# Second layer's experts: the body behind a turn's first branch takes the output products' PSUM banks (sc) instead of the gather's (ob) and the places' (md)

## The chip, the core and the metric

The kernel runs on one core of a Trainium2 chip. Its time is the device time of one execution in microseconds (us). TensorE (PE in the rows) multiplies and transposes into PSUM, eight banks of 128 partitions by 512 fp32 values; VectorE (DVE) and ScalarE (ACT) read the banks; GpSimd (POOL) takes no part in the stretch spoken of here; SyncE (SP) issues the weight loads.

## The reference

Two layers of a hybrid block over 256 latent tokens and 256 context tokens of width 1024. In each layer a mixer of four head groups is followed by a mixture of 16 experts, of which a router gives each token two. The part that matters:

```
for e in range(N_EXPERTS):                       # 16
    a = jax.nn.silu(h @ w_gate[e]) * (h @ w_up[e])
    y = y + gates[..., e:e + 1] * (a @ w_down[e])   # gates are 0 for all but 2 experts of a token
```

`w_gate` and `w_up` are 1024 x 512, `w_down` 512 x 1024, all fp32: 6 MB an expert. In the second layer only the 256 latent tokens go through the experts.

## The kernel before, in words

An expert's tokens are counted on the chip and put into blocks of 64 slots (`BLK`). The second layer (`turns()` within `moe`, lines 1864 to 1933) runs sixteen turns, one expert each, in an order written out by hand on all engines. Every engine reads the expert's count into a register (`cv`). A turn does, in this order on TensorE:

1. the input product of the first block (`mm_in`, L1544, into a bank of tag pj), with the additions of the turn before last (`add`, L1597, tag ob, read by VectorE at L1606) between its parts; ScalarE makes the SiLU of it (`act`, L1550) and VectorE multiplies by the gate (L1551);
2. the first branch, L1882: if the expert has more than 64 tokens, its body gathers a second block (`fetch`, L1515) and makes the input product and the activation of it;
3. in the first twelve turns a quarter of the gather of four experts' first blocks that come later (`four_fetch`, L1100, tag ob), copied out by ScalarE or VectorE;
4. a matmul that finds the places of the block's tokens (`where`, L1575, tag md), compared on VectorE (L1576);
5. four transposes of the activated block (`spin`, L1557, tag tp), copied by ScalarE (L1558);
6. the output product of the turn before (`mm_out`, L1568, tag sc), scaled on VectorE and split on ScalarE and VectorE (`parts`, L1582 to L1587);
7. the second branch, L1920, whose body finishes a second block.

The banks are taken from a pool by tag, in rotation within a tag: `BANKS = {"tp": 1, "md": 1, "pj": 2, "sc": 2, "ob": 2}`, all eight. Semaphores are laid by the framework from what the program's text uses, body or not: who takes a bank after the branch waits for the last reader in the body. Where the body is skipped, each engine, as it comes past the branch, raises its semaphore by what the body would have raised, and does so in its own order, behind the work that it had before the branch.

The weights come in six loads of 1 MB a turn (L183), issued by SyncE as soon as their buffer is free, turns ahead.

Of the kernel before, what the change touches and what calls it, by code (L numbers as in the profile page):

```python
# [123 lines left out]
def hybrid_block_kernel(ctx: ExitStack, tc: tile.TileContext, xin, const, fconst, par, fpar, misc, fng,  # L124
# [12 lines left out]
    def bank(tag="tp"):  # L137
        return psp.tile([P, 512], F32, name="b_" + tag, tag=tag, bufs=BANKS[tag])
# [120 lines left out]
    def C(name, a=0, b=None):  # L259
        at, n = CONST[name]  # L260
        return cst[:, at + a:at + (n if b is None else b)]
# [21 lines left out]
    def copy(dst, src):  # L283
        rr["n"] += 1
        if rr["n"] % 2:
            nc.scalar.activation(dst, src, AF.Copy)
        else:
            nc.vector.tensor_copy(dst, src)
# [796 lines left out]
    def four_onehots(dst, pd, g):  # L1085

        for t in range(dst.shape[1]):
            nc.vector.tensor_tensor(dst[:, t], C("iota")[:, None, :BLK].to_broadcast([P, 4, BLK]),
                                    pd[:, t].rearrange("p (i r) -> p i r", r=4)[:, :, 3 - g:4 - g].to_broadcast([P, 4, BLK]),
                                    op=OP.is_equal)  # L1090
# [305 lines left out]
    def moe(l, cnt, idx, gc, pd, pk, rk, hx, h0, hp):  # L1396
# [5 lines left out]
        with ExitStack() as mctx:  # L1402
# [27 lines left out]
            b = bank()  # L1430
# [61 lines left out]
            def onehot(e, cols, off=None, name=None, into=None):  # L1492

                qs = []
                for t in range(T):
                    q = into[t] if into else ew.tile([P, cols.shape[1]], F32R, name=f"{name}{t}", bufs=1)
                    if off is None:
                        V.tensor_scalar(q, cols, pd[:, t, e:e + 1], None, op0=OP.is_equal)
                    else:
                        V.tensor_scalar(q, cols, off, pd[:, t, e:e + 1], op0=OP.add, op1=OP.is_equal)  # L1500
                    qs.append(q)
                return qs
# [1 line left out]
            def to_slots(h, b):  # L1504
                copy(h.rearrange("p k s -> p (k s)"), b)

            def fetch(oh):

                h = rp.tile([P, 8, BLK], F32, name="hO", tag="h0")
                for j in range(4):  # L1510
                    b = bank("ob")
                    for k in range(2):
                        at = (2 * j + k) * P
                        for i in range(2 * T):
                            nc.tensor.matmul(b[:, k * 256:(k + 1) * 256], lhsT=hx[i % 2][:, i // 2, at:at + P],  # L1515
                                             rhs=oh[i // 2], start=(i == 0), stop=(i == 2 * T - 1))
                    copy(h[:, 2 * j:2 * j + 2], b.rearrange("p (k s) -> p k s", s=256)[:, :, :BLK])
                return h
# [17 lines left out]
            def mm_in(w, h, s0=0, tag="pj", between=None, b=None, ks=range(8)):  # L1536
                b = bank(tag) if b is None else b
                for k in ks:
                    if between:
                        between(k)  # L1540
                    for j in range(2):
                        at = (k % 2) * D + j * 512
                        x = h[k // 4][:, k % 4] if isinstance(h, list) else h[:, k, s0:s0 + BLK]
                        nc.tensor.matmul(b[64 * j:64 * j + 64], lhsT=x,  # L1544
                                         rhs=w[k // 2][:, at:at + 512],
                                         start=(k == 0), stop=(k == 7), tile_position=(0, 64 * j))
                return b

            def act(b, gate, a):
                nc.scalar.activation(a[64:], b[:64], AF.Silu)  # L1550
                V.scalar_tensor_tensor(a[64:], a[64:], gate[64:], b[64:], op0=OP.mult, op1=OP.mult)  # L1551
                return a
# [37 lines left out]
            def add(*blocks, only=None, last=False, banks=None):  # L1590

                for t in range(T) if only is None else only:
                    for h in range(2):
                        cs = slice(h * 512, (h + 1) * 512)
                        b = banks[h] if banks else bank("ob")
                        for i, (st, ohT) in enumerate(blocks):
                            nc.tensor.matmul(b, lhsT=ohT[:, t * P:(t + 1) * P], rhs=st[h],  # L1597
                                             start=(i == 0), stop=(i == len(blocks) - 1))
                        if last:
                            pool = h and t < T - 1  # L1600
                            y = AM[2] if pool and t % 2 == 0 else HE[1].rearrange("p k s -> p (k s)")[:, cs]
                            V.tensor_mul(y, b, g2[t // 2][:, cs])
                            (nc.gpsimd if pool else V).tensor_tensor(xres[t][:, cs], xres[t][:, cs], y, op=OP.add)
                        else:
                            y = xres[t] if l else ACC[t]
                            V.tensor_tensor(y[:, cs], b, y[:, cs], op=OP.add)  # L1606
# [68 lines left out]
            w = aT = owed = None  # L1675
# [184 lines left out]
            def next_count(p):  # L1860

                return nc.values_load(cnt[0:1, TURNS[p]:TURNS[p] + 1], engines=engs, min_val=0, max_val=N)

            def turns():

                w = aT = owed = before = None
                oh1 = onehot(TURNS[0], C("iota2"), off1, name="on")
                cv = next_count(0)  # L1870
                for p, e in enumerate(TURNS):
                    last = p == NE - 1
                    now, nxt = four[p // 4 % 2], four[(p // 4 + 1) % 2]
                    pw, pT, w = w, aT, [main.take("exp", l, 6 * e + q) for q in range(6)]
                    x = [q[:, :, p % 4] for q in now[0]]

                    a1, t1, st1, o1 = AM[(p + 1) % 2], AT[(p + 1) % 2], ST[(p + 1) % 2], OT[(p + 1) % 3]
                    if p % 4 == 0 and p < NE - 4:
                        four_onehots(nxt[1], pd, p // 4 + 1)
                    b0 = mm_in(w, x, between=lambda k: owed and k in (4, 6) and add(owed, only=[k // 2 - 2]))  # L1880
                    a0 = act(b0, gc[:, 0, e:e + 1], AM[p % 2])
                    with tc.If(cv > BLK):  # L1882
                        act(mm_in(w, fetch(oh1), tag="md"), gc[:, 1, e:e + 1], a1)
                    if last:
                        any_ = nc.values_load(cnt[0:1, 16:17], engines=engs, min_val=0, max_val=N)
                    else:
                        main.done(4, 2 if p else 0)
                        onehot(TURNS[p + 1], C("iota2"), off1, into=oh1)
                        if p < NE - 4:
                            four_fetch(nxt[0], hx, nxt[1], [p % 4])  # L1890
                        ncv = next_count(p + 1)
                    o = where(e, OT[p % 3], C("slot", 0, 1), "md")
                    aT = spin(a0, AT[p % 2])
                    if p:
                        b = mm_out(pw, pT, bank("sc"))
                        main.done(2)
                        owed = parts(b, ST[p % 2]), before

                    def second():
                        where(e, o1, C("slot", 1, 2), "md")  # L1900
                        add((parts(mm_out(w, spin(a1, t1)), st1), o1))

                    if last:
                        b = mm_out(w, aT, bank("sc"), lambda f: f > 1 and add(owed, only=[f - 2]))

                        owed = parts(b, st1), o
                        st1 = ST[p % 2]
                        with tc.If(any_ > BLK):
                            with tc.If(cv > BLK):
                                second()  # L1910
                            for q in range(NE):
                                ce = nc.values_load(cnt[0:1, q:q + 1], engines=engs, min_val=0, max_val=N)
                                with tc.If(ce > P):
                                    for i in range(6):
                                        nc.sync.dma_start(w[i], source("exp", l, 6 * q + i))
                                    overflow(q, w, ce, P, a1, t1, st1, o1, into=oh1)
                        add(owed)
                        main.done(6)
                        break
                    with tc.If(cv > BLK):  # L1920
                        second()
                    cv, before = ncv, o
# [215 lines left out]
```

## Time and profile before

| | |
|---|---|
| runs shown | 1346.06, 1339.88, 1345.20 us; median 1345.2 |
| profiled execution | 1349.27 us, of which the span from the first to the last instruction is 1347.1 |
| TensorE busy in the span | 1151.7 us (85%) |
| second layer's experts | from 1060.9 us, the first input product, to about 1338 |
| mean granted TensorE clock | 0.916 |

The time of the profiled execution is 4.1 us over the median of the three runs. Times in rows are us from the start of the span. A line number is that of the kernel's file; most operations of a turn are recorded at the line of a helper. [...] A window's row gives its stretch and length, then busy us and the count of instructions of TensorE, its weight loads, VectorE, ScalarE and GpSimd, and behind them the granted clock, the mean busy share of the 16 DMA engines and GB/s. In a row, `[0.73 <-ACTq L1882]` says that the engine stood idle for 0.73 us before it, and what ended that: here ScalarE's sequencer at the branch.

### The profile page before, as it was taken

The numbers are of one execution on the slowest core, as the hardware profiler recorded it, in microseconds if no ns is written. First come the engines' busy times: TensorE is split into PE (matmuls) and PEld (weight loads), VectorE is DVE, ScalarE is ACT, GpSimd is POOL, SyncE is SP. The second block draws the span as 40 slices with busy tenths as digits, with TensorE's granted clock in tenths as the row PEclk, the third lists the DMA queues.
The fourth block names the chain that finished last, engine by engine and source line by source line (L and its number), as shares of the span: only waits on it lengthen the run. The fifth ranks groups of instructions, "written<-read, shape, count | busy, mean of one in ns | idle before, by whom it ended". The sixth has DMA issues, their size and how long they took to land. (4 is left out here: it accounts for less than half of the span.)

```text
span 1347.1 us, 16575 instructions
## 1 busy us (share of the span) xinstructions
PE 1151.7 (85%) x6205; PEld 644.7 (48%) x6205; DVE 538.8 (40%) x1070; ACT 314.9 (23%) x569; POOL 294.1 (22%) x238
## 2 busy tenths in 40 slices
PE   6799998887899879978898995788878899989984
PEld 2456565556688433323233333667667533333321
DVE  4431967335423530110010038486535444433444
ACT  2422233222222121011111115314424111111111
POOL 4332232222024111111111045534315000000000
PEclk9999998888799788989999996989869899999997
DMA  9485442412571787499999836121136399976951
GB/s 363 181 321 189 157 179 97 146 63 95 217 267 67 287 351 245 128 387 391 384 394 392 327 111 225 63 94 48 63 156 258 123 402 420 418 287 256 420 200 49
DMA packets 48559, 310.61 MB, mean 231 GB/s; under 512 B 6017, under 2 KB 6209, under 8 KB 14096
## 3 DMA queue, kind: packets, MB, share of 16 engines
q1 hardware_dynamic: 41936, 292.77, 55.9%
q0 software_dynamic: 6320, 15.27, 4.4%
q8 instruction: 91, 1.49, 0.4%
q10 hardware_dynamic: 144, 0.52, 0.1%
q14 instruction: 68, 0.56, 0.1%
HBM read 297.99 MB, written 12.32 MB: 230 GB/s over the span
## 5 line engine op out<-in xcount | busy, mean ns | idle before, releaser
L603 POOL TENSOR_TENSOR ws<-w,ws 128x1024 fp32r<-128x1024 f32 x50 | 121.1, 2436 | 218.2 <-ACT ws L602 200.6
L1544 PE MATMUL b_pj<-w,HE 128*64 128x512 f32 x416 | 109.7, 664 | 23.8 <-issue 19.3
L234 PE MATMUL b_pj<-hh,ws 128*128 128x512 f32 (+1 forms) x448 | 122.2, 362 | 1.4 <-POOL ws L603 1.4
L1568 PE MATMUL b_sc<-w,rows 128*64 128x512 f32 x448 | 109.7, 634 | 0.6 <-ACT rows L1558 0.6
L693 DVE SCALAR_TENSOR_TENSOR cacc<-gl,pr,cacc 128x512 f32<-128x512 f32 (+1 forms) x120 | 91.8, 765 | 2.6
L234 PEld LDWEIGHTS b_pj<-hh,ws 128*128 128x128 f32 x448 | 79.5, 198 | 21.1 <-issue 9.7
L234 PE MATMUL b_pj<-hl,ws 128*128 128x512 f32 (+1 forms) x224 | 78.3, 350 | 0.0
L1544 PEld LDWEIGHTS b_pj<-w,HE 128*64 128x64 f32 x416 | 34.6, 150 | 85.7 <-issue 82.5
L602 ACT ACTIVATE ws<-w 128x1024 fp32r<-128x1024 f32 x50 | 52.5, 1052 | 70.2 <-PE b_pj L234 44.6
L277 POOL TENSOR_TENSOR rf<-rf,half 128x1 f32<-128x1 f32 x2 | 1.1, 553 | 300.3 <-DVE rf L276 300.3
L1568 PEld LDWEIGHTS b_sc<-w,rows 128*64 128x64 f32 x448 | 32.7, 145 | 63.5 <-issue 60.7
L1606 DVE TENSOR_TENSOR x<-b_ob,x 128x512 f32<-128x512 f32 x68 | 44.0, 687 | 43.7 <-PE b_ob L1597 43.6
L1451 POOL DMA_INDIRECT sums<-y,rws x19 | 29.8, 1567 | 137.4 <-DVE y L1450 122.3
L1551 DVE SCALAR_TENSOR_TENSOR X<-X,gc,b_pj 64x512 f32<-64x512 f32 x16 | 12.1, 754 | 109.2 <-ACT X L1550 109.2
L1544 PE MATMUL b_pj<-w,hf 128*64 128x512 f32 x224 | 54.0, 619 | 0.9 <-PEq L1920 0.5
L234 PE MATMUL b_md<-w,sT 128*32 128x256 f32 x704 | 53.8, 430 | 1.3 <-DVE mT L313 1.3
L1544 PE MATMUL b_pj<-w,x 128*64 128x512 f32 x224 | 52.9, 601 | 1.0 <-PEq L1920 0.6
L1450 DVE COPY y<-b_sc 128x512 f32<-128x512 f32 x15 | 10.4, 692 | 102.1 <-PE b_sc L1568 61.9
L1597 PE MATMUL b_ob<-st,ohT 128*128 128x512 f32 x76 | 33.1, 504 | 18.9 <-DVE st L1587 11.9
L234 PEld LDWEIGHTS b_pj<-hl,ws 128*128 128x128 f32 x224 | 44.5, 199 | 5.2
L1550 ACT ACTIVATE X<-b_pj 64x512 f32<-64x512 f32 x16 | 9.4, 589 | 158.8 <-PE b_pj L1544 151.2
L1456 POOL DMA_INDIRECT G<-hbuf,idx x15 | 15.2, 1016 | 110.8 <-PE b_ob L1528 61.7
(475 smaller groups left out, 2062.4 us busy)
## 6 DMA issues: line engine op xcount, KB each, us to landing
w<-in_exps_dram SPq DMA_DIRECT2D x168, 1024.0 KB, 12.1
w<-in_ada_dram SPq DMA_DIRECT2D x48, 1024.0 KB, 4.9
w<-in_win_dram SPq DMA_DIRECT2D x16, 1024.0 KB, 6.0
hold<-in_exps_dram SPq DMA_DIRECT2D x12, 1024.0 KB, 18.5
w<-in_wout_dram SPq DMA_DIRECT2D x8, 1024.0 KB, 4.8
hf<-in_exps_dram SPq DMA_DIRECT2D x6, 1024.0 KB, 4.7
cst<-in_exps_dram SPq DMA_DIRECT2D x6, 1024.0 KB, 9.2
pr<-in_par_dram SPq DMA_DIRECT2D x2, 1461.5 KB, 6.2
```

What stands on the lines that cost most here:

```text
L234: nc.tensor.matmul(out_, lhsT=lhsT, rhs=rhs, **kw)
L602: nc.scalar.activation(wh[:, :n], src, AF.Copy)
L603: nc.gpsimd.tensor_tensor(wl[:, :n], src, wh[:, :n].bitcast(F32), op=OP.subtract)
L693: nc.vector.scalar_tensor_tensor(ac, gl[:, :, j:j + L], R("cvw", i * 31 + j, i * 31 + j + 1), ac, op0=OP.mult, op1=OP.add)
L1450: V.tensor_copy(y, b)
L1451: nc.gpsimd.indirect_dma_start(out=sums[:, :], out_offset=bass.IndirectOffsetOnAxis(ap=row, axis=0), in_=y, in_offset=None, bounds_check=1 ...
L1456: nc.gpsimd.indirect_dma_start(out=g, out_offset=None, in_=hbuf[:, :], in_offset=bass.IndirectOffsetOnAxis(ap=ix, axis=0), bounds_check=N ...
L1544: nc.tensor.matmul(b[64 * j:64 * j + 64], lhsT=x, rhs=w[k // 2][:, at:at + 512], start=(k == 0), stop=(k == 7), tile_position=(0, 64 * j))
L1551: V.scalar_tensor_tensor(a[64:], a[64:], gate[64:], b[64:], op0=OP.mult, op1=OP.mult)
L1568: nc.tensor.matmul(b[64 * j:64 * j + 64], lhsT=aT[:, f, :], rhs=w[4 + f // 2][:, at:at + 512], start=(f == 0), stop=(f == 3), tile_positio ...
L1597: nc.tensor.matmul(b, lhsT=ohT[:, t * P:(t + 1) * P], rhs=st[h], start=(i == 0), stop=(i == len(blocks) - 1))
L1606: V.tensor_tensor(y[:, cs], b, y[:, cs], op=OP.add)
```

## The change

`fetch` gets a tag for its banks, and the body of the first branch in `turns()` gives it sc, for the gather and for the input product behind it. The other caller of `fetch`, for a third block of an expert, keeps ob.

```
-            def fetch(oh):
+            def fetch(oh, tag="ob"):

                 h = rp.tile([P, 8, BLK], F32, name="hO", tag="h0")
                 for j in range(4):
-                    b = bank("ob")
+                    b = bank(tag)
...
                     with tc.If(cv > BLK):
-                        act(mm_in(w, fetch(oh1), tag="md"), gc[:, 1, e:e + 1], a1)
+                        act(mm_in(w, fetch(oh1, "sc"), tag="sc"), gc[:, 1, e:e + 1], a1)
```

The order of instructions stays the same on every engine; what each waits for does not. On TensorE, in turn 3, right behind the first branch (a row is a line, an operation, output and inputs, the output's size; `hxh` and `hxl` are the two halves of the tokens, `ohs` the one-hot choice, `pick` and `pdT` the places' inputs; the names in brackets are the semaphores waited for, DVE, PE, Activation and the load queues):

```order
 L1882 UNCONDITIONAL_BRANCH [waits PE_49]
-L1100 MATMUL b_ob<-ohs,hxh 128x256 [waits DVE_49,PE_49,Activation_49]
+L1100 MATMUL b_ob<-ohs,hxh 128x256 [waits DVE_49]
...
 L1862 TENSOR_LOAD cnt
-L1575 MATMUL b_md<-pdT,pick 128x256 [waits DVE_49,Activation_49]
-L1557 MATMUL b_tp<-cst 128x64 x4
-L1568 MATMUL b_sc<-w,rows 64x512 [waits DMAHW5_49]
+L1575 MATMUL b_md<-pdT,pick 128x256
+L1557 MATMUL b_tp<-cst 128x64 [waits DVE_49]
+L1557 MATMUL b_tp<-cst 128x64 x3
+L1568 MATMUL b_sc<-w,rows 64x512 [waits DMAHW5_49,DVE_49,PE_49]
```

The gather keeps one wait, for an addition of VectorE ahead of the branch; the places' matmul has none left; the transposes now carry the wait for the activation, and the output product takes on the wait for the branch. Turns 13 to 16 read the same, without the gather.

On VectorE, at the same branch in turn 1, the body's own operations (`hO` is the gathered block, `cst` the activated one, `gc` the gates):

```order
 L1882 COMPARE_AND_BRANCH
-L288 COPY hO<-b_ob 128x128 x2
-L1551 SCALAR_TENSOR_TENSOR cst<-cst,gc,b_md 64x512
+L288 COPY hO<-b_sc 128x128 x2
+L1551 SCALAR_TENSOR_TENSOR cst<-cst,gc,b_sc 64x512
 L1882 UNCONDITIONAL_BRANCH x2
 L1500 TENSOR_SCALAR on_11681<-cst,off_11667,pd 128x256
```

Nothing but the banks that they read has moved there; on ScalarE it is the same, and GpSimd and SyncE have no difference.

## Rows read from the trace of the kernel before

**Rows 1.** Windows: us, busy and count per engine, clock, DMA share, GB/s.

```profile
1093.05:1108.16 15.11, 14.22 (x65) 5.41 (x65) 6.61 (x11) 2.83 (x5) 0.00 (x0) 1.00 0.98 392
...
1194.60:1222.84 28.24, 23.29 (x92) 8.26 (x90) 11.90 (x19) 4.47 (x8) 0.00 (x0) 0.88 0.43 173
...
1253.07:1268.18 15.11, 14.22 (x65) 5.41 (x65) 7.22 (x12) 2.23 (x4) 0.00 (x0) 1.00 1.01 420
1268.18:1284.71 16.53, 14.74 (x57) 4.79 (x57) 6.62 (x11) 2.23 (x5) 0.00 (x0) 0.90 1.01 418
1284.71:1301.23 16.52, 14.74 (x57) 4.79 (x57) 6.62 (x11) 2.23 (x4) 0.00 (x0) 0.90 0.72 282
1301.23:1316.06 14.83, 13.04 (x57) 4.39 (x57) 6.62 (x11) 2.24 (x5) 0.00 (x0) 1.00 0.01 2
1316.06:1338.18 22.12, 13.94 (x45) 4.69 (x45) 9.78 (x15) 4.30 (x7) 0.00 (x0) 0.79 0.08 25
```

**Rows 2.** List of waits from 1055 us: total us, times, longest us.

```profile
PE b_ob L1100 <- ACTq L1882: 8.1, 11, 0.8
...
PE b_md L1575 <- DVEq L1882: 6.5, 4, 1.6
...
PE b_pj L1544 <- PEq L1920: 1.3, 8, 0.2
...
PE b_pj L1544 <- DMA w<-in_exps_dram: 0.6, 4, 0.2
```

**Rows 3.** Timeline of turn 3: start us, us, engine, line, operation, count, idle before.

```profile
1091.07 1.94 PE L1544 MATMUL b_pj<-w,hf 128*64 128x512 f32 x8
1093.05 0.59 ACT L1550 ACTIVATE cst<-b_pj 64x512 f32<-64x512 f32 x1 [6.80 <-PE b_pj L1544]
...
1093.67 0.75 DVE L1551 SCALAR_TENSOR_TENSOR cst<-cst,gc,b_pj 64x512 f32<-64x512 f32 x1 [1.45 <-ACTq L1882]
...
1093.74 0.39 PE L1100 MATMUL b_ob<-ohs,hxh 128*128 128x256 f32 x1 [0.73 <-ACTq L1882]
...
1094.59 0.73 DVE L1500 TENSOR_SCALAR on<-cst,off,pd 128x256 fp32r<-128x256 f32 x2 [0.16 <-DVEq L1882]
...
1094.89 0.38 PE L1575 MATMUL b_md<-pdT,pick 16*128 16x256 f32 x1
...
1095.20 0.46 PE L1557 MATMUL b_tp<-cst 64*128 64x64 f32 x4
...
1095.59 0.65 PE L1568 MATMUL b_sc<-w,rows 128*64 128x512 f32 x2
```

**Rows 4.** Timeline of turn 13, which has no gather.

```profile
1266.20 1.94 PE L1544 MATMUL b_pj<-w,x 128*64 128x512 f32 x8
1268.18 0.59 ACT L1550 ACTIVATE cst<-b_pj 64x512 f32<-64x512 f32 x1 [6.80 <-PE b_pj L1544]
...
1268.81 0.75 DVE L1551 SCALAR_TENSOR_TENSOR cst<-cst,gc,b_pj 64x512 f32<-64x512 f32 x1 [1.45 <-ACTq L1882]
...
1269.77 0.35 PE L1575 MATMUL b_md<-pdT,pick 16*128 16x256 f32 x1 [1.63 <-DVEq L1882]
...
1270.04 0.46 PE L1557 MATMUL b_tp<-cst 64*128 64x64 f32 x4
```

**Rows 5.** Line L1515, the body's gather: durations ns, first and last start us.

```profile
L1515 PE MATMUL b_ob<-on,hxh x16: 279/279/388, 1183.6 to 1187.3; 128*128 128x256 f32 x16
```

**Rows 6.** Timeline of turn 9, whose body runs, behind the branch.

```profile
1194.60 0.39 PE L1100 MATMUL b_ob<-ohs,hxh 128*128 128x256 f32 x1
...
1196.24 0.35 PE L1575 MATMUL b_md<-pdT,pick 16*128 16x256 f32 x1 [0.42 <-DVE cst L1551]
```

**Rows 7.** Timeline of SyncE's loads from 1060 us: start us, us, load, count.

```profile
1123.36 21.59 SPq L183 DMA_DIRECT2D w<-in_exps_dram  x12
...
1268.27 22.36 SPq L183 DMA_DIRECT2D w<-in_exps_dram  x10
```

**Rows 8.** Weight tiles w from 1060 to 1300 us: issue to landing.

```profile
DMA to landing us min/median/max: 7.9/10.7/14.3
```

## The prediction

> **What bounds the kernel now.** I read first the windows, one for each turn of the second layer's experts [rows 1]. A turn is one expert of sixteen; a window runs from the SiLU of its first block to that of the next turn, so the first row is turn 3, the second turn 9, the third turn 12 and the last four are turns 13 to 16. What the reader is to see: the plain turns 3 and 12 last 15.11 us, TensorE is busy 14.22 us of that at clock 1.00, VectorE and ScalarE less than half. TensorE bounds these turns, and about 0.9 us of a turn is TensorE standing still. Turns 4 to 8, 10 and 11 are like them.
>
> The list of waits says where it stands still [rows 2]. Eleven waits of TensorE's gather (L1100) for ScalarE at the branch L1882 make 8.1 us, 0.74 each; four waits of the matmul of the places (L1575) for VectorE at the same branch make 6.5 us, 1.63 each. For the weights it waits 0.6 us in all, so the loads are not the bound.
>
> The timeline of turn 3 shows the wait itself [rows 3]. The input product ends at 1091.07 + 1.94 = 1093.01. ScalarE's SiLU ends at 1093.64, and only then, at 1093.74, does the gather start, although it reads nothing that the SiLU makes. It waits because the body behind the branch, skipped in this turn, would have used both ob banks, and ScalarE and VectorE report the body as done when they come past the branch, each behind its half of the activation. Turn 13 shows the other form [rows 4]: no gather follows, and the places' matmul, whose bank (md) the body would have used, waits until VectorE is past the branch, 1.63 us.
>
> **The body hardly runs.** Its own gather (L1515) stands in the trace with one body's matmuls, from 1183.6 to 1187.3, in turn 9 [rows 5], the one whose window is 28.24 us [rows 1]. What the change does to the work in the body therefore counts once; what it does to the waits behind the branch counts sixteen times.
>
> **The change, part by part.** No instruction is added or removed; banks and waits change.
>
> *Gather, turns 1 to 12 without 9 (eleven).* It now waits for an addition into x that VectorE made before the activation (in turn 3 the pair at L1606 ended before 1093.01, since the activation follows it). What stays is the pause of TensorE's own passing of a branch. The trace has it where no bank is at stake: behind the second branch, L1920, eight times for 1.3 us, 0.16 each [rows 2]. I take 0.16. The bounds are 0 (behind the body, in turn 9, the gather starts with no idle noted [rows 6]) and the present 0.74. Then in turn 3: gather at 1093.17, places 1.15 later at 1094.32, transposes (L1557) at 1094.63, output product at 1095.02 instead of 1095.59. The transposes need VectorE's half of the activation, which ends at 1093.67 + 0.75 = 1094.42: in time by 0.2. Sum: 8.1 - 11 x 0.16 = **6.3 us**.
>
> *Places, turns 13 to 16.* The md bank is no longer touched by the body, so the places' matmul goes as soon as TensorE is past the branch, but the transposes behind it still need the activation. In turn 13 that ends at 1268.81 + 0.75 = 1269.56; a hop between engines takes 0.10 (ScalarE's end 1093.64, gather 1093.74 [rows 3]), so the transposes start at 1269.66 and not 1270.04: 0.38 a turn. Below lies 0; above, the whole 1.63 - 0.16 cannot be had because of the activation. Sum: 4 x 0.38 = **1.5 us**.
>
> *Turn 9.* The places' matmul waited 0.42 for the body's activation, which held md [rows 6]; now that sits in an sc bank: **0.4 us**. The body's fetch and product move to sc, whose last reader (the scaling of the earlier turn's output) is long done: nothing there.
>
> *The new wait.* The output product (L1568) writes an sc bank, so it now waits for all three engines to be past the branch. Behind it on TensorE stands the next turn's whole input product, and everything waits for that. What covers it: VectorE's first operation past the branch starts at 1094.59 [rows 3], so the release comes no later than 1.58 after the input product's end; the output product is due at 2.01. Cost 0, with 0.43 to spare. In turn 13 the release came 1.63 after [rows 4] and the output product is due at about 1.9.
>
> *The clock.* [...] The 1.63 us wait stands in all four turns, and turn 16, with the program's end behind it, shows 0.79, so I count a fall in three of the four; the plain turns with waits of 0.74 show none. After the change TensorE would run the places' matmul of turn 13 from 1268.14 + 0.16 = 1268.30 for 0.27 us, and then stand until 1269.66: 1.1 us, between the two cases. I take half of 3 x 1.7: **2.5 us**, bounds 0 and 5.1. [...]
>
> **The sum.** 6.3 + 1.5 + 0.4 = 8.2, with the clock 10.7. The profiled execution took 1349.3 us (span 1347.1 and 2.2 around it) and would come to 1338.6. It lies 4.1 above the median of the runs shown, 1345.2, which differ by 6.2 among themselves. Seen from the median: **1334.5 us**; without the clock 1337.0, with all of it 1331.9.
>
> **Rivals.**
>
> *The loads become the bound.* A turn reads 6 x 1.049 = 6.29 MB. Turn 12 draws 420 GB/s at a DMA share of 1.01 [rows 1], and at 420 a turn can't be under 14.98; I forecast 14.54. Then the eleven turns give 0.13 each, 1.4 in all, and with 1.5 + 0.4 + 2.5 the time is 1339.4 (1341.9 without the clock). Against it: the loads are ahead. The row of twelve loads from 1123.36 begins with load 39 of 96 (58 from there to the end), the third of turn 7, read in the second half of an input product that ends at 1153.5; with the longest landing, 14.3, it is there at 1137.7 [rows 7, 8], some 11 us early. Eight turns at 0.44 short eat 3.5 of that. And in turn 15's window, in which turn 16's input product runs, nothing is loaded any more (2 GB/s [rows 1]). [...] Chance 0.10.
>
> *The change doesn't do what it says.* The pause could be that of TensorE's branch itself, so that it stays at 0.74 under another name: 1345. For it: every one of the waits stands at L1882. Against it: the branch at L1920 costs 0.16. Chance 0.12.
>
> *Slower, through the new wait.* The output product waits at sc for VectorE's passing of the branch. Up to 2.01 after the input product's end this costs nothing, from 2.58 on (where the output product starts now, 1095.59 - 1093.01) a turn is longer than before, and at 3.0 sixteen turns lose 6.7 us: 1352. In the rows the passing comes at 1.58 and 1.63 at the latest, so it would have to be delayed by 1.4. Chance 0.04.
>
> **Numbers.** The forecast has 0.74. About 0.5%, 6.7 us, is what a measurement of this kernel can tell from no change. Faster by that means below 1338.5: the forecast's share but for its edge, 0.71. Same: the loads, the branch's pause and that edge, 0.25. Slower 0.04. Range: at the low end no pause at all (1.8 more) and the whole clock, 1330.1, and 2 for the spread of the runs, 1328; at the high end into the loads' case, 1341.
>
> **What would show it.** Right: plain turns of about 14.5 us, the eleven waits of L1100 at L1882 gone or 0.16, L1575 without a wait on VectorE, a wait of L1557 on the activation in turns 13 to 16, L1568 without one, the clock above 0.90 in turns 13 and 14. Wrong: plain turns at 15.0 with waits for weights (the loads); L1568 waiting at L1882 (the new wait); the gather idle 0.7 us as before (the branch's own pause); turns 13 to 16 at 0.90 as before (the clock).

## The result and the profile after

| | before | after |
|---|---|---|
| median | 1346.48 us (11 runs, 1339.88 to 1352.72) | **1333.78 us** (11 runs, 1328.41 to 1338.72) |
| ratio of the times | | **0.9915**, 95% interval 0.9895 to 0.9934 |
| profiled execution | 1349.27, span 1347.1 | 1331.17, span 1329.1 |
| first to last SiLU of the second layer's experts | 248.02 | 238.09 |

The forecast was 1334.5. The last line of the table is the stretch that the rest of this text goes by. Two runs far above the others (one of e6 at 2169.62 us, one of the kernel before beside it at 3212.29) were in a slow state and are left out of the medians and ratios below. The executions of one kernel differ by some 10 us among themselves, and much of that lies ahead of this stretch, in work that the change doesn't touch (its first SiLU comes at 1062.3 in one profiled execution of the changed kernel and at 1070.3 in another); the stretch itself repeats to a tenth (238.09 and 238.18 in two profiled executions of the changed kernel). Of the 18.0 us between the two spans, 5.7 lie ahead of the stretch, 9.9 in it and 2.3 behind it.

The windows of the changed kernel, by turn: us, busy time and count of TensorE, its weight loads, VectorE, ScalarE and GpSimd, then granted clock (the mean over the window), DMA share, GB/s. The rows are turn 3, turn 9 behind its body, turns 13, 14 and 15, and turn 16.

```profile
1086.39:1100.89 14.50, 14.19 (x65) 5.40 (x65) 6.62 (x11) 2.83 (x5) 0.00 (x0) 1.00 1.01 419
...
1184.41:1213.67 29.26, 24.89 (x90) 8.56 (x90) 11.90 (x19) 4.46 (x8) 0.00 (x0) 0.83 0.42 174
1257.19:1271.59 14.40, 13.11 (x57) 4.38 (x57) 6.62 (x11) 2.23 (x4) 0.00 (x0) 1.00 1.01 420
1271.59:1285.99 14.40, 13.11 (x57) 4.39 (x57) 6.62 (x11) 2.23 (x4) 0.00 (x0) 1.00 1.00 412
1285.99:1300.39 14.40, 13.11 (x57) 4.39 (x57) 6.62 (x11) 2.23 (x4) 0.00 (x0) 1.00 0.05 18
...
1300.39:1320.20 19.81, 12.38 (x45) 4.28 (x45) 9.83 (x16) 4.37 (x7) 0.00 (x0) 0.90 0.08 29
```

Against [rows 1]: the plain turn went from 15.11 to 14.50, the part of turn 9 behind its body from 28.13 to 29.26 (the row in [rows 1] begins with the gather, 0.11 ahead of the SiLU that the window after begins with), turns 13 and 14 from 16.53 and 16.52 to 14.40 with the clock at 1.00 in place of 0.90, turn 15 from 14.83 to 14.40, and turn 16 from 22.12 to 19.81. One entry goes the wrong way: turn 9 has become longer.

The list of waits of the changed kernel (total us, times, longest), to be read beside [rows 2]:

```profile
PE b_md L1575 <- PEq L1882: 2.3, 4, 0.6
PE b_tp L1557 <- DVEq L1882: 2.3, 4, 0.6
PE b_ob L1100 <- PEq L1882: 2.0, 11, 0.3
PE b_pj L1544 <- PEq L1920: 1.9, 12, 0.2
```

The gather's 8.1 us of waiting for ScalarE are now 2.0 for TensorE's own sequencer, 0.18 each on average. The 6.5 us of the places are 2.3, and the transposes behind them (L1557) wait 2.3 more, now for VectorE, which comes past the branch right behind its half of the activation. No wait of the output product (L1568) at L1882 has come.

The timelines show both forms at their place. Turn 5 of the changed kernel, a plain one:

```profile
1114.75 0.60 PE L1544 MATMUL b_pj<-w,x 128*64 128x512 f32 x2
1115.40 0.59 ACT L1550 ACTIVATE cst<-b_pj 64x512 f32<-64x512 f32 x1 [6.80 <-PE b_pj L1544]
...
1115.51 0.36 PE L1100 MATMUL b_ob<-ohf,hxh 128*128 128x256 f32 x1 [0.16 <-PEq L1882]
...
1116.03 0.76 DVE L1551 SCALAR_TENSOR_TENSOR cst<-cst,gc,b_pj 64x512 f32<-64x512 f32 x1 [1.45 <-ACTq L1882]
...
1116.63 0.38 PE L1575 MATMUL b_md<-pdT,pick 16*128 16x256 f32 x1
...
1116.94 0.46 PE L1557 MATMUL b_tp<-cst 64*128 64x64 f32 x4
...
1117.33 0.20 PEld L1568 LDWEIGHTS b_sc<-w,rows 128*64 128x64 f32 x4
```

The input product ends at 1114.75 + 0.60 = 1115.35; the gather starts 0.16 later, while the SiLU still runs. The transposes at 1116.94 come 0.15 behind the end of VectorE's half of the activation (1116.03 + 0.76 = 1116.79) and have no idle in front of them; the output product's first weights follow at 1117.33, 1.98 after the input product's end. Turn 13, with no gather:

```profile
1257.72 0.35 PE L1575 MATMUL b_md<-pdT,pick 16*128 16x256 f32 x1 [0.57 <-PEq L1882]
1257.82 0.76 DVE L1551 SCALAR_TENSOR_TENSOR cst<-cst,gc,b_pj 64x512 f32<-64x512 f32 x1 [1.45 <-ACTq L1882]
1258.62 0.32 PEld L1557 LDWEIGHTS b_tp<-cst 64*128 64x128 f32 x4 [0.76 <-DVEq L1882]
1258.63 0.46 PE L1557 MATMUL b_tp<-cst 64*128 64x64 f32 x4 [0.56 <-DVEq L1882]
```

The one standstill of 1.63 us [rows 4] has become two of 0.57 and 0.56 with the places' matmul between them.

### The profile page after: what moved, and what is told of

The parts are those of the page before. It is cut to its first block, busy times and chain, and to the rows that moved or that the text cites. A ratio compares the mean times of both kernels' runs of the same rounds, so it can differ in the third digit from the quotient of the medians.

```text
span 1329.1 us, 16569 instructions
## 1 busy us (share of the span) xinstructions
PE 1146.8 (86%) x6205; PEld 644.2 (48%) x6205; DVE 538.7 (41%) x1070; ACT 314.6 (24%) x569; POOL 293.9 (22%) x238
## 5 line engine op out<-in xcount | busy, mean ns | idle before, releaser
L1544 PE MATMUL b_pj<-w,HE 128*64 128x512 f32 x416 | 107.6, 653 | 23.1 <-issue 20.8
L1568 PE MATMUL b_sc<-w,rows 128*64 128x512 f32 x448 | 103.7, 604 | 0.6 <-ACT rows L1558 0.6
L1544 PEld LDWEIGHTS b_pj<-w,HE 128*64 128x64 f32 x416 | 34.1, 149 | 84.5 <-issue 82.3
L1568 PEld LDWEIGHTS b_sc<-w,rows 128*64 128x64 f32 x448 | 31.1, 138 | 58.3 <-issue 56.5
L1544 PE MATMUL b_pj<-w,hf 128*64 128x512 f32 x224 | 53.9, 618 | 1.0 <-PEq L1920 0.6
L1544 PE MATMUL b_pj<-w,x 128*64 128x512 f32 x224 | 52.9, 601 | 1.0 <-PEq L1920 1.0
```

What stands on the lines that cost most here:

```text
L1544: nc.tensor.matmul(b[64 * j:64 * j + 64], lhsT=x, rhs=w[k // 2][:, at:at + 512], start=(k == 0), stop=(k == 7), tile_position=(0, 64 * j))
L1568: nc.tensor.matmul(b[64 * j:64 * j + 64], lhsT=aT[:, f, :], rhs=w[4 + f // 2][:, at:at + 512], start=(f == 0), stop=(f == 3), tile_positio ...
```

## The experiments

All are edits of the changed kernel. The first four ran on one chip, the next four on another, the last two on a third, each group beside its own runs of the kernel before (medians 1346.78, 1347.89 and 1349.04). "Turns" are from SiLU to SiLU.

| run | median us (runs) | ratio to before, 95% | plain turn | turns 13, 14, 15 | first to last SiLU |
|---|---|---|---|---|---|
| before | 1346.48 (11) | | 15.11 | 16.53, 16.52, 14.83 | 248.02 |
| after | 1333.78 (11) | 0.9915 [0.9895, 0.9934] | 14.51 | 14.40, 14.40, 14.40 | 238.09 |
| e1_gather_half | 1341.88 (12) | 0.9959 [0.9930, 0.9988] | 14.83 | 16.53, 14.82, 16.53 | 244.14 |
| e2_places_half | 1339.35 (12) | 0.9951 [0.9928, 0.9974] | 15.11 | 14.41, 14.40, 14.41 | 243.59 |
| e3_md_last_four | 1340.37 (12) | 0.9953 [0.9931, 0.9975] | 14.51 | 14.84, 16.52, 14.84 | 241.10 |
| e4_no_body | 1324.11 (6) | 0.9833 [0.9799, 0.9868] | 14.40 | 14.40, 14.40, 14.40 | 224.13 (less of turn 9) |
| e5_sc_out_first | 1338.26 (10) | 0.9920 [0.9893, 0.9947] | 14.51 | 14.80, 14.80, 14.80 | 239.28 |
| e6_pj_out_first | 1333.44 (5) | 0.9898 [0.9859, 0.9937] | 14.76 | 14.04, 14.35, 14.04 | 238.72 |
| e7_pj | 1335.12 (8) | 0.9915 [0.9880, 0.9949] | 14.76 | 14.65, 14.66, 14.65 | 240.32 |
| after_again | 1334.14 (6) | 0.9889 [0.9848, 0.9931] | 14.51 | 14.39, 14.40, 14.40 | 238.18 |
| e8_sc_pj | 1334.04 (6) | 0.9882 [0.9860, 0.9903] | 14.51 | 14.05, 14.05, 14.04 | 237.13 |
| e9_sc_md | 1334.46 (6) | 0.9901 [0.9880, 0.9921] | 14.50 | 13.79, 13.78, 13.79 | 236.32 |

**Each half alone.** e1 moves the gather's banks only, e2 the product's only.

```
e1:  act(mm_in(w, fetch(oh1, "sc"), tag="md"), ...)
e2:  act(mm_in(w, fetch(oh1), tag="sc"), ...)
```

> Only the body's gather moves to sc; its input product keeps md. If the waits are the banks' alone: L1100 goes 0.16 us behind the input product as in the changed kernel, but L1575 still waits for VectorE at the branch, about 1.58 us behind the input product, so a plain turn ends up near 14.9 us (0.2 saved, not 0.6), turns 13 to 16 keep their 1.63 us wait and their falls of the clock, and the whole saves 2 to 3 us: about 1344, ratio 0.998. If the gather's wait alone were the cost, plain turns fall to 14.5 and the time to about 1340.

> Only the body's input product moves to sc; its gather keeps ob. If the waits are the banks' alone: L1100 waits 0.74 us as before and plain turns stay at 15.1, while turns 13 to 16 become those of the changed kernel, 14.40 us with the clock at 1.00: 4 x 0.4 us and up to three falls of 1.7 us, so 2 to 7 us in all, about 1340.5, ratio 0.9955. If the falls of the clock do not hang on the wait of L1575, turns 13 and 14 stay at 16.1 with clock 0.90 and the time is about 1344.5.

The turns of both came out as expected; e1's time of 1341.9 lies 2 us under the expected 1344, half of it in turn 9 (27.18 us behind its body, 28.13 before). Windows of e1, turns 3, 13, 14 and 15, and below them one row of its list of waits:

```profile
1090.71:1105.54 14.83, 14.22 (x65) 5.40 (x65) 6.62 (x11) 2.83 (x5) 0.00 (x0) 1.00 1.01 413
1262.54:1279.07 16.53, 14.74 (x57) 4.78 (x57) 6.61 (x11) 2.23 (x5) 0.00 (x0) 0.90 1.00 413
1279.07:1293.89 14.82, 13.04 (x57) 4.39 (x57) 6.61 (x11) 2.23 (x4) 0.00 (x0) 1.00 0.87 339
1293.89:1310.42 16.53, 14.74 (x57) 4.80 (x57) 6.62 (x11) 2.23 (x4) 0.00 (x0) 0.90 0.01 1
```

```profile
PE b_md L1575 <- DVEq L1882: 9.3, 13, 1.6
```

In plain turns the gather's half saves only 0.28: of the 9.3 us, four long waits as before make 6.5, and nine new ones share the other 2.8. The gather comes earlier, and then the places' matmul waits for VectorE's passing of the branch in its stead. Windows of e2, turns 3 and 13:

```profile
1087.96:1103.08 15.12, 14.22 (x65) 5.40 (x65) 6.62 (x11) 2.83 (x6) 0.00 (x0) 1.00 0.95 386
1263.32:1277.73 14.41, 13.11 (x57) 4.39 (x57) 6.61 (x11) 2.24 (x5) 0.00 (x0) 1.00 1.01 417
```

The product's half alone saves nothing in plain turns, since the gather's wait still covers it, and all that the change saves in turns 13 to 15, where no gather is. So in plain turns 0.28 and 0 alone are 0.60 together: two waits in a row at the same branch, the gather's for ScalarE and the places' for VectorE, of which the second shows only when the first is gone.

**The clock.** e3 gives the body's product md again in turns 13 to 16 alone. e5 keeps sc, but puts the output product ahead of the places and the transposes there, so that the new wait on sc has no cover.

```
e3:  act(mm_in(w, fetch(oh1, "sc"), tag="md" if p >= NE - 4 else "sc"), ...)
e5:  +  if p >= NE - 4:
     +      b = mm_out(pw, pT, bank("sc"))
     +      main.done(2)
        o = where(e, OT[p % 3], C("slot", 0, 1), "md")
        aT = spin(a0, AT[p % 2])
```

> The changed kernel, but in turns 13 to 16 the body's product takes md again, so that L1575 waits there as before. Plain turns 14.5. If the wait of 1.63 us brings the falls of the clock: turns 13 to 15 at 14.8 us without and 16.5 with a fall, two or three falls in the four turns, and 3 to 7 us more than the changed kernel, 1337 to 1341. If the falls were chance that the change merely shifted away: 1.6 us more, about 1335.5, with clock 1.00 in all four.

> The changed kernel, but in turns 13 to 16 the output product of the turn before stands ahead of the places' matmul and the transposes, so that the new wait on sc has no cover. If that wait is real and only covered in the changed kernel: L1568 waits 1.63 us for VectorE at L1882 in each of the four turns, which take 14.8 us instead of 14.40, and 16.5 where the clock falls (two or three times): 1.6 to 7 us over the changed kernel, 1336 to 1341. If the wait is nothing, the order costs nothing or gains: 14.40 or less and 1334 or less.

Turns 14 of both on TensorE. First e3, its window and its timeline:

```profile
1279.17:1295.69 16.52, 14.74 (x57) 4.79 (x57) 6.61 (x11) 2.23 (x4) 0.00 (x0) 0.90 0.88 363
```

```profile
1280.75 0.35 PE L1575 MATMUL b_md<-pdT,pick 16*128 16x256 f32 x1 [1.63 <-DVEq L1882]
1281.03 0.47 PE L1557 MATMUL b_tp<-cst 64*128 64x64 f32 x4
1281.42 1.97 PE L1568 MATMUL b_sc<-w,rows 128*64 128x512 f32 x6
```

And e5:

```profile
1277.73:1292.53 14.80, 13.07 (x57) 4.59 (x57) 6.52 (x11) 2.23 (x4) 0.00 (x0) 1.00 0.96 397
```

```profile
1279.27 3.65 PE L1568 MATMUL b_sc<-w,rows 128*64 128x512 f32 x16 [1.58 <-DVEq L1882]
1282.85 0.38 PE L1575 MATMUL b_md<-pdT,pick 16*128 16x256 f32 x1
```

With the places' 1.63 us back, e3 has a turn at 0.90 again, 1.7 us longer than its neighbours at 14.84. e5 stands still about as long, 1.58, ahead of the output product, and the clock stays at 1.00 in all of turns 13 to 15: the falls that I expected there did not come. Over the profiled executions, of the turns 13 to 15 that had the places' wait of 1.63, five of nine ran at 0.90, 1.7 us longer (before two, e1 two, e3 one); of those without it, e5 apart, none of 24 is as much longer. Turn 16 goes the same way: its first 24 matmuls of L1568 take 7.07 us in before and 5.37 in the changed kernel, and ScalarE's wait there for the scaled output (L1586) is 5.63 us in before, e1 and e3, and 3.94 in the changed kernel, e2, e4 and e7, which have the same order. With turn 16, eight of twelve such waits are followed by a fall, and in e5 none of four. So a wait of that length alone doesn't bring the fall, as far as four turns of one profiled execution can show it; whether the small matmuls that follow it in e3 and not in e5 make the difference, or the moment at which the wait comes, was not taken apart further. By the medians, e5 lies 4.1 us above the changed kernel beside it (after_again), of which the profiled stretch shows 1.1; the intervals of the two overlap, and falls in e5's other executions aren't excluded.

**How much of the pause is the branch.** e4 leaves out the first branch and its body, and with it the second block of the one expert that has more than 64 tokens.

```
-                    with tc.If(cv > BLK):
-                        act(mm_in(w, fetch(oh1, "sc"), tag="sc"), ...)
```

> The changed kernel without the first branch and its body: it leaves out the second block's input product and activation of the experts with more than 64 tokens (turn 9 alone here). Turn 9 loses the body's 11 us. If the 0.18 us that L1100 still waits in the changed kernel is the price of TensorE's passing of the branch, it goes, plain turns come to 14.3 and the whole to about 1320; if it is something else, plain turns stay at 14.5 and the whole comes to about 1322.5. If the loads are close behind, plain turns stop at 15.0 or weights are waited for.

Windows of e4, turns 3 and 13, and a row of its waits:

```profile
1094.91:1109.30 14.39, 14.21 (x66) 5.39 (x67) 6.61 (x11) 2.82 (x5) 0.00 (x0) 1.00 1.01 418
1252.25:1266.65 14.40, 13.07 (x58) 4.39 (x58) 6.62 (x11) 2.23 (x4) 0.00 (x0) 1.00 1.01 418
```

```profile
PE b_tp L1557 <- DVE cst L1551: 4.7, 4, 1.2
```

A plain turn is 14.39, between the two expectations, and the median of 1324.1 lies above both: of 15.11 - 14.39 = 0.72 us that the branch cost in a plain turn before, the change took 0.61, and 0.11 is left. In turns 13 to 16 nothing is left: without any branch they are 14.40 too, since the transposes wait 1.2 us for the activation. That is one standstill in one piece, and no fall of the clock follows it in any of the four turns.

The 0.11 left is not shown to be the price of one instruction. In turn 5 the gather's copy (L286) starts 1.14 us behind the start of the SiLU in e4 and 1.34 in the changed kernel: without the branch the gather comes 0.20 earlier. The transposes' copy (L1558) starts 2.00 and 2.10 behind it, so about half of that is gone by then, and in e4 the transposes' weight load waits for VectorE's half of the activation in all sixteen turns, 8.2 us in all. The branch's own records at L1882 in the kernel before last 0.045 us on ScalarE's sequencer, 0.056 on VectorE's and 0.24 on TensorE's, in the median.

**Another bank.** e7 is the changed kernel with the input products' banks (pj) for the body; e6 is e7 with e5's order.

```
e6, e7:  act(mm_in(w, fetch(oh1, "pj"), tag="pj"), ...)
```

> The same order in turns 13 to 16, but the body behind the first branch takes the two banks of the input products (pj), so that nothing right behind the branch waits for it. Turns 13 to 16 then lose the two waits of 0.57 us each and keep 0.16: 13.4 us a turn, 4 us in all, about 1330, ratio 0.988, clock 1.00. If the next input product or its additions wait for the scaled output instead, the turns stay at 14.40 and the time at 1334.

> The changed kernel with pj for the body in place of sc and the order as it was. If the banks matter only by who waits right behind the branch, this is the changed kernel again: plain turns 14.5, turns 13 to 16 at 14.40, about 1334, L1568 without its wait for VectorE; turn 9 may lose 1 us, since its body needs the bank that its own activation still reads. If the wait on sc costs something after all, plain turns come under 14.5 and the time under 1333.

> The changed kernel once more beside these three on their chip: 14.5 us for plain turns, 14.40 for turns 13 to 16 without a fall of the clock there, ratio near 0.9915. If the missing falls of the clock were chance in its first profile, one or more of turns 13 to 16 shows 16 us at 0.90 here.

Both missed. The turns of e7 are 0.25 longer than the changed kernel's, which ran again beside it and repeated itself (turns 10 and 12 are 0.5 longer, which was not explained, and turn 9 is shorter, see below). In e6 the output product still stands 0.57 us at the branch, where I expected 0.16:

```profile
PE b_sc L1568 <- PEq L1882: 2.3, 4, 0.6
```

That and the 0.25 make the 13.4 expected to 14.06; 14.04 was measured. The timeline of e7 at the start of an input product, and its line L1544 in the same stretch:

```profile
1122.62 1.03 PE L1568 MATMUL b_sc<-w,rows 128*64 128x512 f32 x4
...
1124.07 1.08 PE L1544 MATMUL b_pj<-w,x 128*64 128x512 f32 x4 [0.42 <-DMA w<-in_exps_dram]
```

```profile
L1544 PEld LDWEIGHTS b_pj<-w,x x8: 133/137/137, 1124.0 to 1125.0; 128*64 128x64 f32 x8
L1544 PE MATMUL b_pj<-w,x x6: 592/593/644, 1124.1 to 1125.0; 128*64 128x512 f32 x6
L1544 PEldq EVENT_SEMAPHORE  x2: 51/51/51, 1123.8 to 1124.0; - x2
```

TensorE stands for 0.42 us where the changed kernel stands for 0.16, and the row names a load of weights. That would be the loads' rival come true. But the gap is the same 0.42 whatever name it has, the load's in eight turns of e7 and that of TensorE's own sequencer at the second branch (L1920) in five:

```profile
PE b_pj L1544 <- DMA w<-in_exps_dram: 3.4, 8, 0.4
PE b_pj L1544 <- PEq L1920: 2.1, 5, 0.4
```

And in front of the first weights stand two semaphore instructions of TensorE's own sequencer that the changed kernel doesn't have at this place; as I read them, the input product now has to collect the body's readers of pj one after the other. e8 and e9 were made to tell these two apart. Both have sc in turns 1 to 12 and e5's order in turns 13 to 16, where the body has pj (e8) or md (e9).

```
+                        tg = "sc" if p < NE - 4 else "pj"     # e9: "md"
+                        act(mm_in(w, fetch(oh1, tg), tag=tg), ...)
```

> The changed kernel, but in turns 13 to 16 the body takes the banks of the input products (b_pj) and the output product stands ahead of the places and the transposes; turns 1 to 12 as in the changed kernel. Theory (with b_pj in the body, the next input product has to collect the body's readers of that bank, in two more semaphore instructions of TensorE's sequencer ahead of its first weights, 0.25 us a turn): plain turns 14.51 again, turns 13 to 15 as they were with b_pj and this order, 14.04, 14.35, 14.04, no fall of the clock there; about 1 us less than the changed kernel, 1332.8. Rival (the 0.25 us of a plain turn with b_pj were late weights, since the trace names the loads there): which body bank the last four turns have cannot matter to turns 2 to 8, so it too gives 14.51 there, but then turns 13 to 16, whose weights are long on chip, should show no gap of 0.41 us ahead of the next input product.

> As the run with b_pj in the last four turns, but there with the bank of the places (b_md) for gather and product of the body. The places then wait for the body's passing, but stand behind the output product, so that the wait should be over before they come. Theory: plain turns 14.51; turns 13 to 15 without the two more semaphore instructions ahead of the input product: 14.04 less 0.25, about 13.8 each; no fall of the clock; about 2 us less than the changed kernel, 1331.8. Rival (the pause at the branch itself is what is left, whatever the bank and the order): 14.4 a turn as in the changed kernel, 1333.8. If a standstill ahead of the places still brings falls of the clock: 15.5 in every other turn.

Windows of e9, a plain turn and turns 13 and 14:

```profile
1103.80:1118.31 14.51, 14.19 (x65) 5.39 (x65) 7.98 (x14) 2.23 (x4) 0.00 (x0) 1.00 1.01 417
1260.10:1273.89 13.79, 13.07 (x57) 4.60 (x57) 6.52 (x11) 2.23 (x4) 0.00 (x0) 1.00 1.02 421
1273.89:1287.67 13.78, 13.07 (x57) 4.60 (x57) 6.52 (x11) 2.23 (x4) 0.00 (x0) 1.00 1.02 419
```

The plain turns of both are 14.51 again, turns 13 to 15 14.05 with pj and 13.79 with md: 0.26 between kernels that differ in the body's bank alone, as in the plain turns of e7. The gap ahead of the input product is there in e8, 0.4 us in each of these three turns, and the row names VectorE this time:

```profile
PE b_pj L1544 <- DVE ohT L1576: 1.2, 3, 0.4
```

So the 0.25 comes and goes with the body's bank, and not with a late load: three names stand for the same gap. The two semaphore instructions, 0.051 us each, were read in the one gap of e7 shown above. (Of e6's turns, 14.35 in the middle of two of 14.04 was not explained.) e9 against e5 prices the new wait without its cover: the same order, 14.80 with sc and 13.79 with md, 1.0 us a turn. Over its whole stretch e9 is 1.8 us shorter than the changed kernel (236.32 to 238.09); by the medians, 1334.46 and 1333.78 on different chips, the two can't be told apart, and e9 is no proven improvement.

## Why the prediction was right, step by step

The forecast of 10.7 us from the profiled execution stands beside 9.9 in the stretch and 2.3 behind it, 12.3 in all, and 12.7 by the medians. That the time came within 0.7 us is in part luck: the saving was 2.0 short, and the median that it was taken from, 1345.2 of three runs, lies 1.3 below that of eleven. Among the terms, the clock was 2.8 too small and turn 9 1.5 too good, and these too offset each other in part. The terms:

| term | forecast | measured |
|---|---|---|
| gather, eleven plain turns | 6.3 | 6.4 (0.47 in turn 1, 0.45 in turn 2, 0.60 to 0.62 in the others) |
| places, turns 13 to 16 | 1.5 | 1.7 (four times the 0.43 of turn 15, which had no fall of the clock before) |
| turn 9 | 0.4 | -1.1 |
| the new wait | 0 | 0 |
| the clock, turns 13 to 16 | 2.5 | 5.3 (what is left of the gains beside the 0.43: 1.7 each in turns 13 and 14, 1.9 in turn 16) |

*Gather.* The 0.16 taken from the second branch was measured as 0.16 at the first in nine turns, and 0.30 in turns 1 and 2. That this needed both halves was in the forecast as one step (gather, then places 1.15 later, unhindered); e1 shows the step failing when md stays.

*Places.* The bound by the activation is what e4 shows: 14.40 with the change, 14.40 with no branch at all.

*The new wait.* It was forecast as covered with 0.43 to spare, and there is no such wait in the trace. e5 and e9 show that the cover does the work: without it the same wait costs 1.0 us a turn.

*The clock.* The 1.7 us a fall is what e3 shows too, 16.52 in turn 14 at 0.90 between 14.84 and 14.84 at 1.00, and the three falls counted are those of turns 13, 14 and 16; within a fall the granted clock is 0.50 (in the kernel before from 1270.9 to 1274.1, in turn 13). The step "I take half" was the cautious one between its bounds, and the upper bound, 5.1, came true: in turns 13 to 16 two pauses of 0.57 and 0.56 brought no fall in the changed kernel, its second profile, e2 and e7, nor did the one pause of 0.57 in e6, e8 and e9. The 1.1 us of standstill that I had reckoned for the transposes was not one piece either: the places' matmul itself started 0.57 after the input product and not 0.16, and cut it in two. That a standstill of 1.1 us lies between the two cases, and half of the gain with it, is not borne out: e4 has 1.2 us in one piece there and no fall. A fall followed the places' 1.63 us in eight of twelve turns, and none followed e5's 1.58 or the pauses of 0.57 (turns 13 to 16), 0.74 (plain turns of the kernel before) and 1.2 (e4).

*Turn 9.* From SiLU to SiLU it takes 39.11 us before and 40.24 after; the 28.24 us that the prediction calls its window are only the part behind the body. The step was right as a wait and wrong as a time. The places' 0.42 us are gone, but the turn lost more at the lower clock, which the forecast had put at nothing there. The timeline of the changed kernel behind the body of turn 9:

```profile
1186.15 3.65 PE L1568 MATMUL b_sc<-w,rows 128*64 128x512 f32 x16
...
1190.04 0.46 PE L1557 MATMUL b_tp<-cst 64*128 64x64 f32 x4
1192.37 5.35 PE L1568 MATMUL b_ob<-w,rows 128*64 128x512 f32 x16 [1.87 <-ACT rows L1558]
1199.90 0.66 PE L1597 MATMUL b_ob<-st,ohT 128*128 128x512 f32 x1 [2.18 <-DVE st L1587]
```

Sixteen matmuls that take 3.65 us at the full clock take 5.35 behind the 1.87 us wait for the transposes' copy: 1.7 more, with a granted clock of 0.50 from 1193.3 to 1196.6. With 1.00 outside the falls and 0.50 within, the windows' means say that the turn spent 29.26 x 0.17 x 2 = 9.9 us at the lower level, and before 28.24 x 0.12 x 2 = 6.8 [rows 1]; half of the 3.1 is 1.6, which less the 0.4 is about the 1.1 that it lost. The kernel before has the same wait at this place and no fall behind it; its fall comes later in the turn, 0.50 from 1209.4 to 1216.1:

```profile
1203.13 3.65 PE L1568 MATMUL b_ob<-w,rows 128*64 128x512 f32 x16 [1.88 <-ACT rows L1558]
```

This goes with the kernel and hardly with chance. The part behind the body takes 29.26 to 29.32 us in all six profiled executions with gather and product in sc there (the changed kernel twice, 0.83 both times, e3, e5, e8, e9), 28.13 in the kernel before, at 0.88, 28.36 in e2, and 26.76 to 27.18 in e1, e6 and e7 (0.94 in e7). With pj for the body, e6 and e7 take 38.4 us for the whole of turn 9, 1.8 less than the changed kernel. Why the clock falls where it does stays open.

*The rivals.* The loads did not bind: a turn of 14.51 takes 6.29 MB, 433 GB/s, and the loads brought 419, so the lead was eaten at about 0.5 us a turn, but TensorE's waits for weights stayed at 0.2 us in all. The branch's own pause is 0.18 and not 0.74, so the second rival is out; in turns 13 to 16, with no gather behind the branch, that pause is 0.57, for which no run shows the reason. The third needed the cover of the new wait to fail, which only e5 brought about.

## What to carry to other kernels

With semaphores laid as here, a body that hardly ever runs still holds its PSUM banks, for whoever takes them next waits until every engine that reads them in the body has passed the branch (here 0.74 us in a plain turn and 1.63 in the last four); give it the banks whose next taker comes last, and check that the work between is longer than the slowest engine's way to the branch. Where several waits at one branch stand in a row, price them together: removing the first shows the second, and each half alone may be worth little or nothing (here 0.28 and 0 us a plain turn, and 0.60 together). And where a wait ends with a name that doesn't fit, such as a load that is always exactly 0.42 us late, look for more semaphore instructions ahead of it before believing the name.

## What was not expected of the hardware

- With the input products' banks in the body, the gap ahead of the next input product is 0.4 us and not 0.16, and a turn is 0.25 to 0.26 us longer: e7 against the changed kernel, e8 against e9. The two more semaphore instructions read there in e7 last 0.051 us each.
- A standstill of 1.6 us ahead of the places' small matmuls was followed by a fall to the lower clock in eight of twelve turns, and ahead of the dense output product in none of four (e5); each fall cost 1.7 us.
- Where the standstill was cut in two of 0.57 and 0.56 us, no fall of the clock came in turns 13 to 16, and that gave more than half of what these four turns gained: 5.3 of 7.0 us.
